# From the second superblock on: token sums of squares as split products with a block of ones and a diagonal, and z gates of two attentions placed elsewhere

## The chip, the cores and the metric

The kernel runs on one core of a Trainium2 chip. The core has a matrix engine (TensorE, PE in the profile, with its weight loads listed apart as PEld), a vector engine (VectorE, DVE), an activation engine (ScalarE, ACT), a general engine (GpSimd, POOL) and a queue processor that here only issues transfers (SyncE, SP). Matrix results land in PSUM, everything else lives in SBUF, inputs and outputs in HBM. The metric is the device time of one execution in microseconds: 2292.9 us, the median of three runs before the change (2291.53 to 2294.29).

## What is computed

The reference is one layer of a hybrid decoder on 2048 tokens of width 1024, all in float32. Cut to the parts that bear on the change:

```python
h = rms_norm(x, norm_g)
p = h @ w_in                       # split into r,k,v,w,a,z_a | q,sk,sv,z_b | xq,z_c | gates
y_a = rwkv7_mix(...)   * silu(z_a) # 8 heads x 64
y_b = sliding_window_sink_attn(...) * silu(z_b)   # 8 q heads x 64, window 128
y_c = memory_cross_attn(...)        * silu(z_c)   # 4 heads x 128, 256 memory tokens
merged = sum(sigmoid(gate_i) * (y_i @ w_proj_i))
x = x + merged @ w_out
# inside rwkv7_mix, per head of 64 channels:
kk = k * k_k;  kk = kk / max(norm(kk), 1e-12)
# inside both attentions, per head (64 or 128 channels):
q = q * rsqrt(mean(q*q) + eps) * g
```

So three places need, per token and head, a sum of squares over the head's channels: the RWKV keys, the queries of the windowed attention, and the queries of the cross attention. (The windowed keys and the memory keys need one too; the change leaves those alone.)

## The kernel before

Tokens go in four superblocks of 512 (`sb` 0 to 3). Activations are kept transposed, channels on the 128 partitions and the 512 tokens along the row. Each projection of `h` to 128 channels (`proj`, L462) is a sum of 24 matmuls of 128 by 128 by 512: float32 operands are split into a high part in the type float32r and a remainder in the same type, and three products high-high, high-low and low-high are added (`gemm3`, L425). The split weights (tiles `whl`) come from HBM: in superblock 0 the raw weights are loaded, split by ACT (L411) and DVE (L412) and written back to a kept copy; in later superblocks the kept copy is loaded (L407).

In each superblock two streams of work are woven. `stream_r` is the RWKV branch: two groups of two head pairs, each group `rwkv_prep` twice, then `rwkv_inverse` (a serial loop on DVE, L754 to L756), then `rwkv_chain` (eight dependent steps). `stream_f` is all the rest: four `cross_head`, `swa_kv`, four `swa_pair` woven with the first output projections (`merge(2)`), `merge(1)`, and eight gates. After both come the split of the RWKV outputs, `merge(0)` and `output`.

The order in which the program writes these steps isn't the order in which an engine runs them. `order` (L276) takes all instructions, estimates each one's time by a table of its own (`cost_PE`, `cost_DVE` and so on), and lays them out by list scheduling: an engine takes, of the instructions that are ready at that time, the one that was written first (its rank, with corrections). That order is then fixed for each engine. Buffers are taken in the order written: each pool of tiles with one name has a fixed number of places, and a tile can be opened only when it is first in its pool's queue (`room`, L197). The pools that matter here are `g2` (11 places of 128 by 512, used by both attentions, by the z gates and by the output), `gt` (2 places, used by the gates of the merges), `rt` (6 places, the scratch of the RWKV stream), and in PSUM `mm` (2 places, all projections), `as_` (2 places, sums and scores of the attentions) and `rw` (2 places, the RWKV stream).

A token's sum of squares is made like this: ACT squares the 128 by 512 tile, and `tok_stat` (L468) takes each of four 128-token slices of the squares as the stationary operand in plain float32 and multiplies it by a narrow constant, `bones` (128 by 2, one column for each half of the partitions) or `ones1` (128 by 1). The results have tokens on the partitions. In `rwkv_prep` (L666 to L674) four small DVE instructions place them by head into `dk` and clamp them. In `cross_head` (L898 to L902) and `swa_pair` (L995 to L999) one DVE copy brings them to `rs`, and POOL makes the inverse root (`rpow`, L391).

The z gate of a head is `silu2` (L869): a projection, a tanh on ACT and one DVE instruction, into a `g2` tile. In `cross_head` it stands after the product with the values (L938), in `swa_pair` after the products with the values (L1056).

Of the kernel before, what the change touches and what calls it, by code (L numbers as in the profile page):

```python
# [9 lines left out]
F32 = mybir.dt.float32  # L10
F32R = mybir.dt.float32r
BF16 = mybir.dt.bfloat16
I32 = mybir.dt.int32
AF = mybir.ActivationFunctionType
ALU = mybir.AluOpType
AX = mybir.AxisListType
# [3 lines left out]
TB = 512  # L20
NG = 11
NRT = 6
SCRATCH = 1024
RAW = 3
C = 64
NC_ = TB // C
# [7 lines left out]
B_R, B_K, B_V, B_WA, B_ZA, B_Q, B_SK, B_SV, B_ZB, B_XQ, B_ZC, B_G = 0, 4, 8, 12, 13, 17, 21, 22, 23, 27, 31, 35  # L34
# [250 lines left out]
def build(tc, A, nsb=4):  # L285
    nc = tc.nc
    es = ExitStack()
    V, S, G, PE = nc.vector, nc.scalar, nc.gpsimd, nc.tensor

    def pool(name, bufs, **kw):  # L290
        return es.enter_context(tc.tile_pool(name=name, bufs=bufs, **kw))
# [5 lines left out]
    rp = pool("rp", 1)  # L297
    yp = pool("yp", 4)
    mp = pool("mp", 9)
    gp_ = pool("gp", NG)  # L300
    bp = pool("bp", 1)
    cp = pool("cp", 1)
    xp = pool("xp", 1)

    def g2(dt=F32, shape=(128, TB)):
        return gp_.tile(list(shape), dt, name="g2")
# [6 lines left out]
    def rw_ps():  # L313
        return ps.tile([128, 512], F32, name="rw", bufs=2)

    def s_ps():
        return ps.tile([128, 512], F32, name="as_", bufs=2)

    def o_ps():
        return ps.tile([128, 512], F32, name="oo", bufs=1)  # L320
# [10 lines left out]
    def const(name, shape, src=None):  # L331
        t = (bp if name == "ident" else fp if name == "eye32" else cp).tile(shape, F32, name="c_" + name)
        nc.sync.dma_start(t, A[name] if src is None else src)
        return t
# [6 lines left out]
    ident = const("ident", [128, 128])  # L341
# [17 lines left out]
    def pcol(name, i=0):  # L359
        o, w = PV[name]  # L360
        return pv[:, o + i:o + i + 1]
# [13 lines left out]
    def dcol(name, i=0):  # L375
        return dv[:, DV[name][0] + i:DV[name][0] + i + 1]
# [27 lines left out]
    def wblock(src, key=None):  # L404
        w = wp.tile([128, 2, 512], F32R, name="whl")
        if key in kept:
            nc.sync.dma_start(w.bitcast(F32), kept[key])  # L407
            return w[:, 0], w[:, 1]
        raw = wp.tile([128, 512], F32, name="raw", bufs=RAW)
        nc.sync.dma_start(raw, src)  # L410
# [51 lines left out]
    def proj(blk, hT, n=TB):  # L462
        o = mm_ps()
        gemm3(o[:, :n], [(w, (hT[0][:, k, :n], hT[1][:, k, :n])) for k, w in enumerate(wtiles(A["w_in"][blk], 8, ("in", blk)))])
        return o


    def tok_stat(sq, nh, ntile, out):  # L468
        rhs = bones if nh == 2 else ones1
        for i in range(ntile):  # L470
            PE.matmul(out[:, i * nh:(i + 1) * nh], sq[:, i * 128:(i + 1) * 128], rhs, start=True, stop=True)

    ones2 = bp.tile([128, 128], F32R, name="ones2")
    S.activation(ones2.rearrange("p (a b) -> p a b", a=2), bones.unsqueeze(2).to_broadcast([128, 2, 64]), AF.Copy)
    ones1 = cp.tile([128, 1], F32, name="ones1")
    V.memset(ones1, 1.0)

    def bcast_T(out, st, nh, ntile):

        w = 128 // nh  # L480
        rep = tmp()[:, :ntile * 128]
        V.tensor_copy(rep.rearrange("p (a b) -> p a b", b=w), st[:, :ntile * nh].unsqueeze(2).to_broadcast([128, ntile * nh, w]))
        for i in range(ntile):
            PE.transpose(out[:, i * 128:(i + 1) * 128], rep[:, i * 128:(i + 1) * 128], ident)
# [127 lines left out]
    def chunks(t):  # L612
        return t.rearrange("p (c t) -> p c t", t=C)

    def shift(o, blk, mu, omu, sb, tag, bufs=1):
        t = rp.tile([128, TB], F32, name=tag, bufs=bufs)
        S.activation(t, o, AF.Copy, scale=omu)
        V.scalar_tensor_tensor(t[:, 1:], o[:, :TB - 1], mu, t[:, 1:], op0=ALU.mult, op1=ALU.add)
        V.scalar_tensor_tensor(t[:, 0:1], carry[sb % 2][:, blk:blk + 1], mu, t[:, 0:1], op0=ALU.mult, op1=ALU.add)
        V.tensor_copy(carry[1 - sb % 2][:, blk:blk + 1], o[:, TB - 1:TB])  # L620
        return t

    def tmp(tag="rt", bufs=NRT):
        return rp.tile([128, TB], F32, name=tag, bufs=bufs)

    EV, OD = slice(0, 64), slice(64, 128)
# [3 lines left out]
    def rwkv_prep(p, i, Z, dk, Nc, sb, hT, lwla, group):  # L630
# [11 lines left out]
        k = shift(kp, B_K + p, pcol("mu_k", p), dcol("omu_k", p), sb, "rk_")  # L642
# [20 lines left out]
            pend.pop(0)()  # L663

        yield 10.317
        sq = tmp()  # L666
        S.activation(sq, k, AF.Square, scale=pcol("k_k", p))
        st = rw_ps()
        tok_stat(sq, 2, 4, st)
        sums, own = st[:, :8].rearrange("p (a e) -> p a e", e=2), dk[:, i].rearrange("p (a o) -> p a o", o=2)  # L670
        for e, h in ((0, EV), (1, OD)):
            for o, at in ((0, EV), (1, OD)):
                V.tensor_scalar(own[h, :, o], sums[at, :, e], 1e-24, None, op0=ALU.max)
        V.reciprocal(dk[:, i], dk[:, i])  # L674
        G.tensor_copy(AB[:, :, C:], gmask[:, C:].unsqueeze(1).to_broadcast([128, NC_, C]))
        G.tensor_tensor(AB[:, :, :C], gmask[:, :C].unsqueeze(1).to_broadcast([128, NC_, C]), dk[:, i].unsqueeze(2).to_broadcast([128, NC_, C]), op=ALU.mult)
# [189 lines left out]
            pend.append(rest)  # L866
        yield 10.587

    def silu2(blk, hT):  # L869

        o = proj(blk, hT)
        t = g2()
        S.activation(t, o, AF.Tanh, scale=0.5)
        V.scalar_tensor_tensor(t, t, 1.0, o, op0=ALU.add, op1=ALU.mult)
        return t
# [10 lines left out]
    def cross_head(h, sb, hT, yh, yl):  # L886
        km = rp.tile([128, 2, M], F32R, name="km", bufs=2)
        nc.sync.dma_start(km.bitcast(F32), Kd[h])
        vm = rp.tile([128, 2, 128], F32, name="vm", bufs=2)
        nc.sync.dma_start(vm, Vd[:, :, h * 128:(h + 1) * 128])  # L890
        o = proj(B_XQ + h, hT)
        qh, ql = g2(F32R), g2(F32R)
        S.activation(qh, o, AF.Copy)
        V.tensor_tensor(ql, o, qh.bitcast(F32), op=ALU.subtract)
        sq = g2()
        S.activation(sq, o, AF.Square)
        yield 1.717
        st = s_ps()  # L898
        tok_stat(sq, 1, 4, st)
        rs = xp.tile([128, 8], F32, name="st8", bufs=2)  # L900
        V.tensor_copy(rs[:, :4], st[:, :4])
        rpow(rs[:, :4], rs[:, :4], 128 * EPS)  # L902
        mx = xp.tile([128, 8], F32, name="mx", bufs=2)
        sps = []
        for t2 in range(2):
            sp = s_ps().rearrange("p (a m) -> p a m", a=2)
            for i in range(2):
                tk = slice((2 * t2 + i) * 128, (2 * t2 + i + 1) * 128)
                gemm3(sp[:, i], [((qh[:, tk], ql[:, tk]), (km[:, 0], km[:, 1]))])
            V.tensor_reduce(mx[:, 2 * t2:2 * t2 + 2], sp, axis=AX.X, op=ALU.max)  # L910
            sps.append(sp)
        V.scalar_tensor_tensor(mx[:, :4], mx[:, :4], -1.0, rs[:, :4], op0=ALU.mult, op1=ALU.mult)
        prs = []
        for t2 in range(2):
            pr = g2(shape=(128, 2, M))
            for i in range(2):
                q = 2 * t2 + i
                S.activation(pr[:, i], sps[t2][:, i], AF.Exp, scale=rs[:, q:q + 1], bias=mx[:, q:q + 1],
                             accum_out=mx[:, 4 + q:5 + q])
            prs.append(pr)  # L920
        dn = xp.tile([128, 8], F32, name="dn", bufs=2)
        V.tensor_scalar(dn[:, :4], mx[:, 4:], 2.0, None, op0=ALU.mult)
        V.reciprocal(dn[:, :4], dn[:, :4])
        yield 5.667
        oo = o_ps()
        for t2 in range(2):
            pt = s_ps().rearrange("p (k i t) -> p k i t", k=2, i=2)
            for i in range(2):
                q = 2 * t2 + i
                V.tensor_scalar(prs[t2][:, i], prs[t2][:, i], dn[:, q:q + 1], None, op0=ALU.mult)  # L930
                for kt in range(2):
                    PE.transpose(pt[:, kt, i], prs[t2][:, i, kt * 128:(kt + 1) * 128], ident)
            pts = g2(shape=(128, 2, 256))
            S.activation(pts.rearrange("p k t -> p (k t)"), pt.rearrange("p k i t -> p (k i t)"), AF.Copy)
            for kt in range(2):
                PE.matmul(oo[:, t2 * 256:(t2 + 1) * 256], vm[:, kt], pts[:, kt], start=kt == 0, stop=kt == 1)  # L936
        yield 3
        z = silu2(B_ZC + h, hT)  # L938
        V.tensor_tensor(z, oo, z, op=ALU.mult)
        split_y(z, yh, yl, "c", h, sb)  # L940
        yield 6.427
# [40 lines left out]
    def swa_pair(j, sb, hT, yh, yl):  # L982
        o = slice(sb * TB, (sb + 1) * TB)
        qp = proj(B_Q + j, hT)
        sq = g2()
# [7 lines left out]
            V.tensor_tensor(q[l], qg[h], q[h].bitcast(F32), op=ALU.subtract)  # L993
        yield 5.067
        st = s_ps()  # L995
        tok_stat(sq, 2, 4, st)
        rs = xp.tile([128, 8], F32, name="st8", bufs=2)
        V.tensor_copy(rs, st[:, :8])
        rpow(rs, rs, 64 * EPS)  # L999
        g = j // 2  # L1000
        mx = xp.tile([128, 4, 4], F32, name="mxs", bufs=2)
# [28 lines left out]
        V.tensor_scalar(dn, dn, 2.0, None, op0=ALU.mult)  # L1030
        V.reciprocal(dn, dn)
        yield 4
        Ps = []
        for b in range(4):
            m0 = m0s[b]
# [17 lines left out]
                    behind(m, prev or last, not prev)  # L1053
                    prev = m
        yield 4
        z = silu2(B_ZB + j, hT)  # L1056
        V.tensor_tensor(z, ops_, z, op=ALU.mult)
        split_y(z, yh, yl, "b", j, sb)
        yield 6
# [54 lines left out]
    def x_norm(sb):  # L1114
        t = hT_tiles()
        norm_T(4, pcols("norm_g"), *t, x0)
        return t
# [32 lines left out]
    hT = x_norm(0)  # L1150
# [3 lines left out]
    for sb in range(nsb):  # L1154
# [51 lines left out]
        if rb is not None:  # L1206
            hT = x_cols(sb + 1, rb)
# [94 lines left out]
```

## Time and profile before

| | |
|---|---|
| median of three runs | 2292.9 us |
| profiled execution, its own time | 2291.46 us |
| its span, first to last instruction | 2289.7 us |
| PE busy | 2251.8 us, 98% |
| PEld busy | 1832.9 us, 80% |
| DVE busy | 1481.7 us, 65% |
| ACT busy | 901.1 us, 39% |
| POOL busy | 149.5 us, 7% |
| mean granted TensorE clock | 0.995 |

The busy time of an engine is the union of its instructions' times. A matmul's end is modelled, and neighbours overlap: a dense matmul's record lasts some 0.39 us, but the next one starts 0.23 us after it. So what a matmul costs the engine is read from start to start in the timeline, and its record's length is not its cost. A float32 matmul leaves two records, so that four instructions of `tok_stat` show as eight. In a timeline row the first number is the start and the second the length, in us, of all the instructions merged into the row. In a row of a group of instructions the last two numbers are busy time in us and mean ns of one.

### The profile page before, as it was taken

Reading aid. Unit: us, or ns where it says so; the run is one execution under the profiler, and the core shown is the slowest. Engines: PE = TensorE matmul, PEld = TensorE weight load, DVE = VectorE, ACT = ScalarE, POOL = GpSimd, SP = SyncE. Lnnn points to the kernel's source line nnn. Section 1 sums busy time; section 2 is a strip of 40 time slices with the busy share of each in tenths; the row PEclk is TensorE's granted clock in tenths of the full one; section 3 lists DMA queues with packets and bytes.
Section 4 is the critical chain, followed back from the end, with each engine's and each line's share of the span. In section 5 each row is a group of like instructions: output and inputs, shape, how many; then the busy total and the mean of one; then the engine's idle time right before and its main releaser. Section 6 shows DMA issues by size and latency. Waiting matters only on the chain.

```text
span 2289.7 us, 37168 instructions
## 1 busy us (share of the span) xinstructions
PE 2251.8 (98%) x13900; PEld 1832.9 (80%) x13900; DVE 1481.7 (65%) x3798; ACT 901.1 (39%) x1971; POOL 149.5 (7%) x209
## 2 busy tenths in 40 slices
PE   8999999999999999999999999999999999999999
PEld 6878778778788788878888878887887887887887
DVE  7799789774458766953435966784244696686312
ACT  6654564545243443433214344332222434434210
POOL 1000110000000010000000001000000001000000
PEclk9999999999999999999999999999999999999999
DMA  7766556589834344446773433445675434343555
GB/s 241 265 210 230 174 178 222 208 288 335 312 135 159 128 140 152 152 155 232 236 254 125 152 122 135 149 148 186 230 251 184 152 131 165 120 153 117 210 193 192
DMA packets 146227, 430.56 MB, mean 188 GB/s; under 512 B 16641, under 2 KB 21121, under 8 KB 146049
## 3 DMA queue, kind: packets, MB, share of 16 engines
q1 hardware_dynamic: 129920, 398.83, 50.4%
q10 hardware_dynamic: 16128, 29.37, 3.8%
q8 instruction: 110, 1.80, 0.3%
q14 instruction: 69, 0.56, 0.1%
HBM read 333.24 MB, written 94.90 MB: 187 GB/s over the span
## 4 chain that ended last, share of the span: by engine, by line
PE 82%; DVE 10%; DMA 3%; ACT 2%; issue 2%; POOL 2%; SPq 0%; ACTq 0%; DVEq 0%; POOLq 0%
PE mm L429 20%; PE mm L431 20%; PE mm L430 19%; PE rw L706 2%; PE rw L827 1%; DVE whl L412 1%; PE oo L1052 1%; PE rw L820 1%; PE mm L1100 1%; PE oo L936 1%; PE mm L1098 1%; PE mm L1099 1%; PE rw L812 1%; POOL var L398 1%; DMA g<-in_x 1%
## 5 line engine op out<-in xcount | busy, mean ns | idle before, releaser
L429 PE MATMUL mm<-hH,whl 128*128 128x512 f32 x1888 | 753.3, 399 | 0.6 <-ACT gt L1065 0.6
L431 PE MATMUL mm<-hH,whl 128*128 128x512 f32 x1888 | 750.9, 398 | 0.0
L430 PE MATMUL mm<-hL,whl 128*128 128x512 f32 x1888 | 749.1, 397 | 0.0
L431 PEld LDWEIGHTS mm<-hH,whl 128*128 128x128 f32 x1888 | 355.6, 188 | 71.7 <-issue 0.7
L429 PEld LDWEIGHTS mm<-hH,whl 128*128 128x128 f32 x1888 | 355.9, 189 | 70.7 <-ACT gt L1065 1.2
L430 PEld LDWEIGHTS mm<-hL,whl 128*128 128x128 f32 x1888 | 355.7, 188 | 69.1 <-issue 0.5
L411 ACT ACTIVATE whl<-raw 128x512 fp32r<-128x512 f32 x178 | 112.3, 632 | 173.6 <-PE mm L431 98.2
L412 DVE TENSOR_TENSOR whl<-raw,whl 128x512 fp32r<-128x512 f32 x178 | 124.5, 701 | 62.3 <-ACT whl L411 61.2
L429 PE MATMUL mm<-yh,whl 128*128 128x512 f32 x384 | 152.0, 396 | 0.8 <-DVE g L1080 0.7
L430 PE MATMUL mm<-yl,whl 128*128 128x512 f32 x384 | 152.0, 396 | 0.0
L431 PE MATMUL mm<-yh,whl 128*128 128x512 f32 x384 | 150.8, 393 | 0.0
L818 ACT ACTIVATE SP<-Z,Pl 64x64 f32<-64x64 f32 x256 | 89.0, 348 | 117.2 <-DVE Z L828 113.6
L754 DVE STREAM_SHUFFLE ibc<-Nc 128x496 f32<-128x496 f32 (+30 forms) x248 | 113.7, 474 | 0.0
L755 DVE TENSOR_TENSOR ibc<-ibc,Yi 128x496 f32<-128x496 f32 (+30 forms) x248 | 104.9, 423 | 4.2
L1027 ACT ACTIVATE g<-g,mxs,st 128x256 f32<-128x256 f32 (+1 forms) x128 | 74.9, 588 | 79.2 <-DVE mxs L1020 78.9
L1080 DVE SCALAR_TENSOR_TENSOR g<-g,mm 128x512 f32<-128x512 f32 x32 | 21.9, 686 | 128.3 <-PE mm L431 128.3
L756 DVE TENSOR_TENSOR Yi<-Yi,ibc 128x496 f32<-128x496 f32 (+30 forms) x248 | 104.0, 419 | 1.4
L828 DVE SCALAR_TENSOR_TENSOR Z<-rw,Pl,SP 64x64 f32<-64x64 f32 x224 | 63.4, 283 | 44.3 <-PE rw L827 40.7
L429 PEld LDWEIGHTS mm<-yh,whl 128*128 128x128 f32 x384 | 72.1, 188 | 16.9 <-DVE g L1080 1.3
L430 PEld LDWEIGHTS mm<-yl,whl 128*128 128x128 f32 x384 | 72.2, 188 | 14.6
L431 PEld LDWEIGHTS mm<-yh,whl 128*128 128x128 f32 x384 | 72.1, 188 | 14.3
L824 DVE TENSOR_TENSOR Z<-rw,dk 64x128 f32<-64x128 f32 x128 | 36.8, 288 | 64.6 <-PE rw L820 54.5
(1815 smaller groups left out, 3718.3 us busy)
## 6 DMA issues: line engine op xcount, KB each, us to landing
whl<-k SPq DMA_DIRECT2D x486, 512.0 KB, 3.3
k<-whl SPq DMA_DIRECT2D x162, 512.0 KB, 3.2
raw<-in_w_in SPq DMA_DIRECT2D x118, 256.0 KB, 3.7
g<-in_x ACTq DMA_DIRECT2D x32, 256.0 KB, 4.3
out<-g ACTq DMA_DIRECT2D x32, 256.0 KB, 4.0
raw<-in_w_proj SPq DMA_DIRECT2D x24, 256.0 KB, 3.7
rt<-in_x ACTq DMA_DIRECT2D x24, 256.0 KB, 4.9
rt<-in_xt ACTq DMA_DIRECT2D x24, 256.0 KB, 5.7
```

The source lines that it names most:

```text
L411: S.activation(w[:, 0], raw, AF.Copy)
L412: V.tensor_tensor(w[:, 1], raw, w[:, 0].bitcast(F32), op=ALU.subtract)
L429: PE.matmul(out, lh, rh, start=i == 0, stop=False)
L430: PE.matmul(out, lh, rl, start=False, stop=False)
L431: PE.matmul(out, ll, rh, start=False, stop=i == n - 1)
L706: m = PE.matmul(g[:, c], BK[h, c0 + c], Q[h, c0 + c], start=True, stop=True)
L754: V.stream_shuffle(bc[:, :, :w], N_[:, :, s + 1:], [s] * 32)
L755: V.tensor_tensor(bc[:, :, :w], bc[:, :, :w], Y[:, :, s:s + 1].to_broadcast([128, n, w]), op=ALU.mult)
L756: V.tensor_tensor(Y[:, :, s + 1:], Y[:, :, s + 1:], bc[:, :, :w], op=ALU.add)
L818: S.activation(SP[h, i], Z[h, i, e, c], AF.Copy, scale=g[4][h, c:c + 1])
L828: upds = [V.scalar_tensor_tensor(Sst[h, g[0]] if c == NC_ - 1 else Z[h, i, e, c + 1], pS[h, i, e], g[4][h, c:c + 1], SP[h, i], op0=ALU.mul ...
L1027: S.activation(prs[b][:, i, m0:], prs[b][:, i, m0:], AF.Exp, scale=r2[:, b, i:i + 1], bias=mx[:, b, i:i + 1], accum_out=mx[:, b, 2 + i:3 + i])
```

## The change

A new constant `FIRST = 1` selects superblocks 1 to 3; superblock 0 keeps the old sums. In the selected ones each of the three places makes its sums with two new helpers. `spread_sums` splits the squares into a high and a low float32r tile (one ACT copy, one DVE subtraction) and multiplies a constant block of ones (`ones2`, block diagonal by halves, or the new `onesw`, all ones) as the stationary operand by both, 512 tokens wide, so that each partition of the result row holds the sum over its head for every token. To have tokens on partitions again, `half_sums` multiplies the result by a repeated 64-wide identity (`eye64`) and sums over each 64 tokens; in `cross_head` four instructions do the same with the 128-wide identity in one go each, a multiplication with an accumulated sum. `swa_pair` then needs four small copies to place the halves.

In all four superblocks, the z gate of `swa_pair` is written before the probabilities are transposed, and the z gate of `cross_head` takes its tile from `gt` instead of `g2`.

```diff
+FIRST = 1
...
+    onesw = bp.tile([128, 128], F32R, name="onesw")
+    S.activation(onesw, ones1.to_broadcast([128, 128]), AF.Copy)
+    eye64 = cp.tile([128, 64], F32, name="eye64")
+    V.tensor_tensor(eye64, ident[:, :64], ident[:, 64:], op=ALU.add)
+
+    def spread_sums(out, w, sq, hi, lo):
+
+        S.activation(hi, sq, AF.Copy)
+        V.tensor_tensor(lo, sq, hi.bitcast(F32), op=ALU.subtract)
+        PE.matmul(out, w, hi, start=True, stop=False)
+        PE.matmul(out, w, lo, start=False, stop=True)
+
+    def half_sums(d, out, junk):
+
+        j = chunks(junk)
+        V.tensor_tensor(j, chunks(out), eye64.unsqueeze(1).to_broadcast([128, NC_, 64]), op=ALU.mult)
+        V.tensor_reduce(d, j, axis=AX.X, op=ALU.add)
...
@@ rwkv_prep
+        if sb >= FIRST:
+            sq = tmp()
+            S.activation(sq, k, AF.Square, scale=pcol("k_k", p))
+            spread_sums(st, ones2, sq, *(rp.tile([128, TB], F32R, name="rt", bufs=NRT) for _ in range(2)))
+            half_sums(dk[:, i], st, sq)
+            V.tensor_scalar(dk[:, i], dk[:, i], 1e-24, None, op0=ALU.max)
+        else:
...
@@ silu2
-    def silu2(blk, hT):
+    def silu2(blk, hT, t=None):
...
-        t = g2()
+        t = g2() if t is None else t
...
@@ cross_head
+        if sb >= FIRST:
+            spread_sums(st, onesw, sq, *(g2(F32R), g2(F32R)))
+            for i in range(4):
+                tk = slice(i * 128, (i + 1) * 128)
+                V.tensor_tensor_reduce(sq[:, tk], st[:, tk], ident, 1.0, 0.0, ALU.mult, ALU.add, rs[:, i:i + 1])
+        else:
+            tok_stat(sq, 1, 4, st)
+            V.tensor_copy(rs[:, :4], st[:, :4])
...
-        z = silu2(B_ZC + h, hT)
+        z = silu2(B_ZC + h, hT, gp_.tile([128, TB], F32, name="gt", bufs=2))
...
@@ swa_pair
+        if sb >= FIRST:
+            spread_sums(st, ones2, sq, *(g2(F32R), g2(F32R)))
+            d = xp.tile([128, 8], F32, name="dh", bufs=2)
+            half_sums(d, st, sq)
+            for i, h in enumerate((EV, OD)):
+                for o, at in enumerate((EV, OD)):
+                    V.tensor_copy(rs.rearrange("p (b i) -> p b i", i=2)[at, :, i], d.rearrange("p (b o) -> p b o", o=2)[h, :, o])
+        else:
+            tok_stat(sq, 2, 4, st)
+            V.tensor_copy(rs, st[:, :8])
...
         V.reciprocal(dn, dn)
         yield 4
+        z = silu2(B_ZB + j, hT)
         Ps = []
...
         yield 4
-        z = silu2(B_ZB + j, hT)
         V.tensor_tensor(z, ops_, z, op=ALU.mult)
```

More of the change, by code (lines that the diff above doesn't have):

```diff
@@ L665, in rwkv_prep @@
         yield 10.317
-        sq = tmp()
-        S.activation(sq, k, AF.Square, scale=pcol("k_k", p))
         st = rw_ps()
[L669 to L673, printed above, removed]
+        if sb >= FIRST:
[5 more added lines that the diff above has]
+        else:
+            sq = tmp()
+            S.activation(sq, k, AF.Square, scale=pcol("k_k", p))
+            tok_stat(sq, 2, 4, st)
+            sums, own = st[:, :8].rearrange("p (a e) -> p a e", e=2), dk[:, i].rearrange("p (a o) -> p a o", o=2)
+            for e, h in ((0, EV), (1, OD)):
+                for o, at in ((0, EV), (1, OD)):
+                    V.tensor_scalar(own[h, :, o], sums[at, :, e], 1e-24, None, op0=ALU.max)
         V.reciprocal(dk[:, i], dk[:, i])
@@ L898, in cross_head @@
         st = s_ps()
-        tok_stat(sq, 1, 4, st)
         rs = xp.tile([128, 8], F32, name="st8", bufs=2)
-        V.tensor_copy(rs[:, :4], st[:, :4])
+        if sb >= FIRST:
[6 more added lines that the diff above has]
+            V.tensor_copy(rs[:, :4], st[:, :4])
         rpow(rs[:, :4], rs[:, :4], 128 * EPS)
@@ L995, in swa_pair @@
         st = s_ps()
-        tok_stat(sq, 2, 4, st)
         rs = xp.tile([128, 8], F32, name="st8", bufs=2)
-        V.tensor_copy(rs, st[:, :8])
+        if sb >= FIRST:
[6 more added lines that the diff above has]
+        else:
+            tok_stat(sq, 2, 4, st)
+            V.tensor_copy(rs, st[:, :8])
         rpow(rs, rs, 64 * EPS)
```

## The prediction

> **What bounds the kernel now.** I read the page's busy times first, then the busy times by stretch, then who waited for whom on PE.
>
> ```profile
> span 2289.7 us, 37168 instructions
> PE 2251.8 (98%) x13900; PEld 1832.9 (80%) x13900; DVE 1481.7 (65%) x3798; ACT 901.1 (39%) x1971; POOL 149.5 (7%) x209
> PE 82%; DVE 10%; DMA 3%; ACT 2%; issue 2%; POOL 2%; SPq 0%; ACTq 0%; DVEq 0%; POOLq 0%
> ```
>
> PE is busy 98% of the span and holds 82% of the chain that ended last. The stretches tell superblock 0 from the others; the columns are the stretch, its length, and busy time with instruction counts of PE, PEld, DVE, ACT and POOL, then the granted clock and the DMA share.
>
> ```profile
> 60.00:570.00 510.00, 494.89 (x3125) 400.77 (x3124) 408.86 (x1006) 271.02 (x572) 38.90 (x47) 0.98 0.67 233
> 630.00:1125.00 495.00, 493.99 (x3174) 401.74 (x3173) 316.70 (x854) 190.02 (x431) 34.09 (x47) 1.00 0.47 162
> 1185.00:1680.00 495.00, 493.55 (x3173) 401.19 (x3172) 318.06 (x856) 190.79 (x432) 34.11 (x47) 1.00 0.47 162
> 1740.00:2240.00 500.00, 499.02 (x3197) 406.36 (x3196) 310.75 (x839) 180.37 (x409) 31.25 (x41) 1.00 0.44 153
> ```
>
> In superblock 0 PE is idle for 510.00 - 494.89 = 15.1 us, with DVE at 80%. In superblock 1 it is idle for 1.0 us, with DVE at 317 of 495, 64%, and ACT at 38%. The waits of PE from 630 to 2240 us are four rows and 3.1 us in all:
>
> ```profile
> PE rw L856 <- DVE rt L853: 1.6, 3, 0.5
> PE as__16692 L1098 <- DVE g L1105: 0.9, 1, 0.9
> PE mm L429 <- DVE g L1080: 0.4, 1, 0.4
> PE as__11578 L1098 <- DVE g L1105: 0.2, 1, 0.2
> ```
>
> So in the three superblocks where the sums change, PE sets the time almost alone. A microsecond less of work in PE's queue is a microsecond less of span there, as long as the other engines go on feeding it.
>
> **What the old sums cost on PE.** A record's length doesn't tell it, so I take starts. First a sum of `rwkv_prep` and then one of `swa_pair`, in PE's timeline:
>
> ```profile
> 885.49 0.39 PE L429 MATMUL mm<-hH,whl 128*128 128x512 f32 x1
> 885.72 0.39 PE L430 MATMUL mm<-hL,whl 128*128 128x512 f32 x1
> 885.95 0.39 PE L431 MATMUL mm<-hH,whl 128*128 128x512 f32 x1
> 886.18 0.95 PE L471 MATMUL rw<-c_bones,rt 128*128 128x2 f32 x8
> 886.98 0.49 PE L429 MATMUL mm<-hH,whl 128*128 128x512 f32 x1
> 887.31 0.40 PE L430 MATMUL mm<-hL,whl 128*128 128x512 f32 x1
> 887.54 0.40 PE L431 MATMUL mm<-hH,whl 128*128 128x512 f32 x1
> ...
> 905.94 0.39 PE L431 MATMUL mm<-yh,whl 128*128 128x512 f32 x1
> 906.17 0.95 PE L471 MATMUL as__9334<-c_bones,g 128*128 128x2 f32 x8
> 906.98 0.37 PE L1011 MATMUL as__9346<-KsH,g 128*128 128x256 f32 x1
> 907.18 0.28 PE L1011 MATMUL as__9346<-KsL,g 128*128 128x256 f32 x1
> 907.30 0.28 PE L1011 MATMUL as__9346<-KsH,g 128*128 128x256 f32 x1
> ```
>
> Dense matmuls start (886.18 - 885.49)/3 = 0.23 us apart. The eight records of a sum take 886.98 - 886.18 = 0.80 us. The first dense matmul behind them costs more than its neighbours: 887.31 - 886.98 = 0.33 where the next takes 0.23, so 0.10 us is added. In the second place it is 0.81, and 0.20 against 0.12, 0.08 added. A sum thus takes 0.90 us of PE in `rwkv_prep` and 0.89 in the attentions.
>
> **What the new sums cost on PE.** Two dense matmuls of 512 columns from a constant block, and no change between plain float32 and float32r on either side. The same form, already in the kernel with `ones2`, is
>
> ```profile
> L731 PE MATMUL rw<-rt,ones 128*128 128x512 f32 x16 | 6.3, 391 | 0.0
> ```
>
> whose record of 391 ns is that of the dense stream (0.39 above), so I take 0.23 from start to start, 0.46 a sum. Each superblock has 4 + 4 + 4 such sums, three superblocks 12 + 24. Off PE come 12 x (0.90 - 0.46) + 24 x (0.89 - 0.46) = 5.3 + 10.3 = 15.6 us. The count of records falls from 8 to 2 a sum.
>
> The Trainium skill, "TensorE: Matmul & The Clock Gate", section "Back-to-back issue gap", lists about 60 cycles for a matmul of 1 to 64 columns and 518 for one of 512. By that table eight records of two columns would take 8 x 60 = 480 cycles, 0.20 us at its 2.4 GHz, and two wide ones 1036, 0.43 us, so the change would add 36 x 0.23 = 8 us. This trace differs: its eight records take 0.80 us.
>
> **What is added beside PE.** Prices come from rows of the same kind:
>
> ```profile
> L1087 ACT ACTIVATE g<-mB 128x512 fp32r<-128x512 f32 x32 | 20.2, 631 | 45.8 <-DVE mB L1081 42.2 <-DMA rt<-in_xt 3.6
> L1089 DVE TENSOR_TENSOR mB<-mB,g 128x512 fp32r<-128x512 f32 x32 | 22.2, 693 | 6.5 <-ACT g L1087 5.6
> L711 DVE TENSOR_TENSOR AB<-rw,AB 64x512 f32<-64x512 f32 x32 | 22.0, 686 | 7.6 <-PE rw L706 7.1
> L848 DVE TENSOR_REDUCE var<-rt 128x8 f32<-128x512 f32 x16 | 10.6, 682 | 2.1 <-ACT rt L846 2.1
> L673 DVE TENSOR_SCALAR dk<-rw 64x4 f32<-64x4 f32 x64 | 10.2, 159 | 0.9
> L1015 DVE CUSTOM_DVE_ANT_0 g<-as__4381,amask x2: 281/344/406, 393.0 to 393.7; 128x128 f32<-128x128 f32 x1, 128x256 f32<-128x256 f32 x1
> L1015 DVE DVE_READ_ACCUMULATOR2_ANT mxs<- x128: 73/84/103, 206.2 to 2065.2; 128x1 f32 x128
> ```
>
> ACT gets 36 copies of 0.63 = 23 us, 7.6 a superblock. DVE per sum: in `rwkv_prep` 0.69 + 0.69 + 0.68 + 0.16, less the four clamps of 0.16 that go, 1.6 us; in `swa_pair` 0.69 + 0.69 + 0.68 + 4 x 0.16 less a copy, 2.5; in `cross_head` 0.69 + 4 x (0.28 + 0.08) less a copy, 2.0. Four each make 24 us a superblock and 73 in all: DVE goes from 64% to 69% and ACT from 38% to 40% in these stretches. I cost this at nothing in the time, since PE hardly waits for either engine there (3.1 us). If that cover goes, the bound is superblock 0: between 64% and 80% of DVE its idle PE time rises from 1.0 to 15.1 us, 0.9 us a point, so 5 points are 4.4 us a superblock and 13 in all. Superblock 0 also has the weight splits that the others lack, so I take the low end.
>
> The RWKV stream gets longer. A sum of `rwkv_prep` ends some 0.63 + 1.6 - 0.44 = 1.8 us later, 7 us in four of them, and the DVE instructions of the attentions, 18 us, can delay its serial loop. So 7 to 25 us, and how late it may end is seen at the end of superblock 1, where its last product (L863) stands against the first matmul of `merge(0)`:
>
> ```profile
> L863 DVE TENSOR_TENSOR ya<-ya,g x2: 685/686/686, 1048.3 to 1048.9; 128x512 f32<-128x512 f32 x2
> ...
> 1112.75 0.48 PE L429 MATMUL mm<-yh,whl 128*128 128x512 f32 x1
> ```
>
> The slack is 1112.75 - 1049.6 = 63 us, filled on PE by `merge(1)` and the gates. The two to four extra tiles of `rt` and `g2` hold up later ones of their pools; their price is in the same bounds.
>
> **The z gates** move no work onto or off PE: 24 matmuls, a tanh, a DVE product and the two weight loads on SP are issued as before, in all four superblocks. In `swa_pair` the loads and the projection now stand ahead of the probabilities' transposes, and the four `P_` tiles queue behind z in `g2`, so that the copies into them (and the products with the values) can't be made before z's tanh. z's projection runs beside the eight exponentials of the pair: 24 x 0.23 = 5.5 us against 8 x (0.59 + 0.19), 6.3 us, by
>
> ```profile
> L1027 ACT ACTIVATE g<-g,mxs,st 128x256 f32<-128x256 f32 x120 | 71.0, 594 | 77.2 <-DVE mxs L1020 76.9
> L1027 ACT ACTIVATION_READ_ACCUMULATOR g<-g,mxs,st 128x1 f32 x128 | 24.4, 190 | 0.0
> ```
>
> That is a cover, so I take 0. In `cross_head` z leaves `g2`, and `gt` is free then, as its gates come later. The bound on both sides is the largest wait that PE has in superblock 0, for the scaled probabilities of a cross head, which may go or come again:
>
> ```profile
> PE as__1903 L932 <- DVE g L930: 3.5, 1, 3.5
> ```
>
> The three instructions for `onesw` and `eye64` run once, while PE waits for the first inputs; 0, at most 1 us.
>
> **Sum.** 2291.5 (profiled execution) - 15.6 = 2275.9. That execution lies 1.4 us under the median of the runs, so for the median 2292.9 - 15.6 = 2277.3, and I say 2277. Bounds of the unknown terms: + 13 for DVE and the pools, + 1 for the constants, 3.5 either way for the z gates.
>
> **Rivals.**
>
> *DVE eats most of it.* The denser DVE delays the evacuation of the two `mm` places and PE stalls as in superblock 0. For it: DVE peaks, 53 of 60 us in the stretch from 690 to 750. Against it: PE is busy 60.00 of 60 us in that very stretch.
>
> ```profile
> 690.00:750.00 60.00, 60.00 (x326) 50.24 (x326) 53.08 (x137) 23.06 (x53) 4.65 (x7) 1.00 0.46 156
> ```
>
> With half to all of the 13 us, 2284 to 2290.
>
> *The sums hold `as_` too long (slower).* The sum's place is one of two in `as_`, and the scores that follow need both. It is now given back after the split and the DVE products: in `swa_pair` 0.63 + 0.69 + 0.69 where a copy of 0.16 stood, in `cross_head` 0.63 + 0.69 + 1.4; 1.9 and 2.6 us later, 12 x 1.9 + 12 x 2.6 = 54 us over 24 heads. If PE has nothing else in its queue at those places, from 15.6 / 54 = 29% exposed the kernel gets slower, and at half exposed it stands at 2277 + 27 = 2304. For it: at the start of a superblock the weights of a cross head's sum already wait for the square,
>
> ```profile
> 1199.29 0.97 PEld L471 LDWEIGHTS as__11848<-ones,g 128*128 128x128 f32 x8 [0.52 <-ACT g L896]
> ```
>
> and the planned order is fixed, so a late sum holds all behind it. Against it: PE shows no other wait for the attentions in superblocks 1 to 3, and projections stand ready to fill.
>
> *PE pays by columns.* If the old sums cost only their few columns, the change adds two dense matmuls, 36 x 0.46 = 16.6 us, 2309. This is the mechanism behind the skill's table above. The starts of the rows speak against it at every place looked at; 1 in 100.
>
> *More gain.* The z gates and the replanned order take away waits of superblock 0 too, 3.5 to 8 of its 15 us: 2269 to 2273.
>
> **Chances.** The forecast itself, 2274 to 2282: 0.60. DVE eats most: 0.16, of which 0.04 ends within 0.2%. More gain: 0.11. Slower by the `as_` places or another stall of the fixed order: 0.09. Between them, no change: 0.03. By columns: 0.01. A change of 0.2% is 4.6 us, about what a measurement of this kernel can tell from no change: under 2288.3 is faster, over 2297.5 slower. Faster is 0.60 + 0.12 + 0.11 = 0.83, same 0.07, slower 0.10. The range leaves out the slower cases and the ends of the others: 2269 to 2290.
>
> **What would show it.** Right: 72 new matmul records of 128 by 512 with the ones blocks in superblocks 1 to 3, 0.46 us a pair from start to start; PE's busy time down by some 16 us, DVE's up by some 73 to 1555, ACT's by 23 to 924; PE's waits from 630 us on still under 6 us; each later superblock some 5 us shorter. Wrong: PE waits at L1011, at the new sums or at the cross scores adding up to over 10 us; a `merge(0)` that waits for the RWKV stream; or dense pairs that cost more than 0.46 us.

## The result, and the profile after

The changed kernel takes 2283.32 us, median of 6 runs (2281.28 to 2284.49), against 2292.22 for the kernel before in the same comparison: a ratio of 0.9961, 95% interval 0.9948 to 0.9974, 8.9 us less. The forecast was 2277 and 15.6 us less. So the direction held, the time lies in the range of 2269 to 2290, just outside the narrower 2274 to 2282 that had most of the chance, and some 7 us of the expected gain are missing.

The page of the changed kernel, in the lines that answer to those shown of before (a line of `after` lies up to 39 further down: `gemm3` is L430 to L432 now, the new sums' matmuls L487 and L488, the cross heads' transposes L963, silu2's tanh L898 and product L899):

```profile
span 2282.2 us, 36933 instructions
PE 2241.2 (98%) x13684; PEld 1814.2 (79%) x13684; DVE 1541.3 (68%) x3967; ACT 916.9 (40%) x2006; POOL 148.6 (7%) x209
PE 70%; DVE 12%; ACT 3%; DMA 2%; issue 1%; POOL 0%; SPq 0%; ACTq 0%; DVEq 0%; POOLq 0%
```

PE's busy time is down by 10.6 us, where the prediction had some 16, and its records by 216 = 36 x 6, eight records of each old sum for two of each new one. Busy time by stretch, columns as in the prediction:

```profile
60.00:570.00 510.00, 496.94 (x3133) 400.61 (x3133) 410.89 (x1012) 271.49 (x575) 37.48 (x47) 0.99 0.68 236
630.00:1125.00 495.00, 493.16 (x3118) 398.22 (x3117) 337.40 (x911) 196.98 (x444) 34.09 (x47) 1.00 0.50 164
1185.00:1680.00 495.00, 493.17 (x3119) 398.35 (x3118) 342.55 (x919) 199.49 (x448) 34.08 (x47) 1.00 0.50 164
```

DVE is at 337 of 495, 68% in superblock 1, and PE still busy 99.6% of it. PE's waits in superblocks 1 to 3, 630 to 2235 us:

```profile
PE rw L837 <- DVE Z L853: 1.1, 3, 0.4
PE as__8859 L487 <- ACT g L485: 0.8, 1, 0.8
PE as__19199 L487 <- ACT g L485: 0.8, 1, 0.8
PE as__14029 L487 <- ACT g L485: 0.8, 1, 0.8
...
PE rw L761 <- DVE carry L638: 0.7, 3, 0.2
```

All of these waits come to 6.0 us, against 3.1 before. Once a superblock a new sum waits 0.8 us for the copy of its high part. Nothing else of size shows, and yet the gain is short. Where it is missing is seen when the span is cut at the last matmul of each `output`. For superblocks 0 and 1 the rows of that line tell it, since the last matmul there is that of the last `as_` tile; first the kernel before, then the changed one:

```profile
L1100 PE MATMUL as__6424<-whl,mB x8: 389/389/389, 613.0 to 625.4; 128*128 128x512 f32 x8
...
L1100 PE MATMUL as__11578<-whl,mB x8: 389/389/389, 1165.0 to 1178.8; 128*128 128x512 f32 x8
```

```profile
L1139 PE MATMUL as__6428<-whl,mB x8: 389/389/390, 616.3 to 628.3; 128*128 128x512 f32 x8
...
L1139 PE MATMUL as__11638<-whl,mB x8: 389/389/395, 1165.0 to 1178.8; 128*128 128x512 f32 x8
```

Superblock 0 ends 2.9 us later than before, and superblock 1 is 2.9 us shorter, so that both kernels stand at 1178.8. All the gain of the span comes behind that point. Cut so, the profiles of all kernels of this study are (us; each from the timeline's last matmul of `output`, with its record of 0.39 us; one execution each; differences in the text can be off by 0.1 from rounding):

| kernel | sums | cross z in | pair z | sb 0 | sb 1 | sb 2 | sb 3 |
|---|---|---|---|---|---|---|---|
| before | old | g2 | late | 625.8 | 553.4 | 554.5 | 552.4 |
| after | new | gt | early | 628.7 | 550.5 | 550.1 | 549.3 |
| e1_sums_only | new | g2 | late | 626.1 | 553.7 | 554.4 | 552.3 |
| e2_z_only | old | gt | early | 628.7 | 554.6 | 555.9 | 553.5 |
| e3_pair_z_only | old | g2 | early | 619.0 | 555.0 | 555.2 | 553.9 |
| e4_cross_z_only | old | gt | late | 631.1 | 552.2 | 553.4 | 551.6 |
| x1_sums_cross_z | new | gt | late | 633.3 | 547.6 | 549.1 | 547.4 |
| x2_sums_pair_z | new | g2 | early | 621.6 | 554.4 | 554.7 | 553.2 |
| x3_split_by_block | new | gt in 1 to 3 | early in 0 | 621.7 | 547.8 | 548.9 | 547.2 |
| x4_sums_12_places | new | g2 of 12 | late | 656.1 | 554.0 | 553.9 | 552.4 |
| y1_probs_out_of_queue | new | g2, pts in gt | late | 631.8 | 550.9 | 551.2 | 549.7 |
| y2_no_cross_sums | new but in cross | g2 | late | 624.7 | 551.4 | 551.9 | 550.9 |
| y4_diag_twice | new, diagonal twice | gt | late | 632.3 | 552.4 | 550.9 | 549.5 |
| y3_split_all_sums | new in 0 too | gt in 1 to 3 | early in 0 | 640.7 | 548.3 | 549.1 | 547.2 |

Two things tell how far such lengths can be trusted. In superblocks 1 to 3 the granted clock is 1.00 in all of these profiles, and kernels with the same order there agree within 0.7 us (x1, x3 and y3). In superblock 0 executions of one order differ by up to 2.7 us (e3, x2 and x3), so the 2.9 us of the changed kernel are little more than that scatter, though e2, with the same order there, repeats them.

### The profile page after: what moved, and what is told of

It reads as the page before. It is cut to its first block, busy times and chain, and to the rows that moved or that the text cites. A ratio compares the mean times of both kernels' runs of the same rounds, so it can differ in the third digit from the quotient of the medians.

```text
span 2282.2 us, 36933 instructions
## 1 busy us (share of the span) xinstructions
PE 2241.2 (98%) x13684; PEld 1814.2 (79%) x13684; DVE 1541.3 (68%) x3967; ACT 916.9 (40%) x2006; POOL 148.6 (7%) x209
## 4 chain that ended last, share of the span: by engine, by line
PE 70%; DVE 12%; ACT 3%; DMA 2%; issue 1%; POOL 0%; SPq 0%; ACTq 0%; DVEq 0%; POOLq 0%
PE mm L431 17%; PE mm L430 17%; PE mm L432 16%; PE rw L731 1%; DVE ibc L779 1%; PE mm L1139 1%; PE mm L1137 1%; PE mm L1138 1%; PE rw L852 1%; PE oo L1092 1%; DVE ibc L780 1%; PE oo L967 1%; PE rw L845 1%; DVE Yi L781 1%; PE rw L837 1%
## 5 line engine op out<-in xcount | busy, mean ns | idle before, releaser
L430 PE MATMUL mm<-hH,whl 128*128 128x512 f32 x1888 | 751.1, 398 | 4.6 <-DVE g L899 3.8
L432 PE MATMUL mm<-hH,whl 128*128 128x512 f32 x1888 | 747.4, 396 | 0.0
L430 PEld LDWEIGHTS mm<-hH,whl 128*128 128x128 f32 x1888 | 355.7, 188 | 76.7 <-DVE g L899 4.3
L432 PEld LDWEIGHTS mm<-hH,whl 128*128 128x128 f32 x1888 | 355.8, 188 | 68.6
L430 PE MATMUL mm<-yh,whl 128*128 128x512 f32 x384 | 152.8, 398 | 1.4 <-DVE g L1119 1.4
L432 PE MATMUL mm<-yh,whl 128*128 128x512 f32 x384 | 151.3, 394 | 0.0
L1104 ACT ACTIVATE gt<-mm 128x512 f32<-128x512 f32 x64 | 37.8, 591 | 129.3 <-PE mm L432 129.2
L430 PEld LDWEIGHTS mm<-yh,whl 128*128 128x128 f32 x384 | 72.1, 188 | 16.6 <-DVE g L1119 2.5
L432 PEld LDWEIGHTS mm<-yh,whl 128*128 128x128 f32 x384 | 72.1, 188 | 14.8
```

Of the source, the lines that this page charges most:

```text
L430: PE.matmul(out, lh, rh, start=i == 0, stop=False)
L432: PE.matmul(out, ll, rh, start=False, stop=i == n - 1)
L1104: S.activation(t, gp, AF.Tanh, scale=0.5)
```

## The experiments

Each ratio below is to the kernel before as it was measured in the same comparison: 2289.86 us for the kernels e1 to e4, 2291.14 for x1 to x4, and 2290.28 for y1 to y4.

**The parts apart.** The first four kernels do the sums alone, the z gates alone, and each z gate alone. With `FIRST = 4` all superblocks keep the old sums.

```diff
# e1_sums_only: the changed kernel with
-        z = silu2(B_ZC + h, hT, gp_.tile([128, TB], F32, name="gt", bufs=2))
+        z = silu2(B_ZC + h, hT)
# and silu2(B_ZB + j, hT) back behind the products with the values
```

> The sums of the changed kernel, with both z gates as in the kernel before. Superblock 0 then has the instructions of the kernel before, but for two constants. Theory A (the sums bring the whole gain in superblocks 1 to 3, some 10 us, and the z gates lose about 3 us in superblock 0): superblock 0 ends near 626 us as before, and the time is 10 to 13 us under the kernel before. Theory B (the z gates carry part of the gain in the later superblocks): 5 to 8 us under it. Theory C (the z gates do nothing and the 3 us of superblock 0 are the scatter of executions): 9 us under it, as the changed kernel.

Measured: 2293.94 us, ratio 1.0019 (1.0010 to 1.0028). No faster than before, by a kernel with the same 216 fewer matmul records: the runs are 0.2% slower, and the span of the profiled execution is 2290.0 us against 2289.7. None of the three theories had that. Superblock 0 is as before (626.1), and each later one takes the old time to 0.3 us: the sums alone gain nothing.

```diff
# e2_z_only: the changed kernel with
-FIRST = 1
+FIRST = 4
```

> Both z gates as in the changed kernel, all sums as in the kernel before (the two new constants are made and unused). Theory A: 2 to 4 us over the kernel before, all of it in superblock 0. Theory B: 1 to 4 us under it, gained in superblocks 1 to 3. Theory C: within 1 us of it.

Measured: 2295.91 us, ratio 1.0025 (1.0017 to 1.0034). Superblock 0 loses the 2.9 us of the changed kernel, and the later ones lose 1.1 to 1.4 each, which no theory had. Neither part gains, and both together do. Theory B is right in that the z gates carry a part, but not as an addition: they let the sums gain. On top of them the sums bring 4.0, 5.8 and 4.2 us a superblock, 14.0 in all, near the forecast of 15.6.

```diff
# e3_pair_z_only: e2_z_only with the cross gate's tile from g2 again
# e4_cross_z_only: e2_z_only with the pair's z gate late again
```

> Only the z gate of the windowed attention is written ahead of the transposes; the cross gate's tile and all sums as before. If the loss of superblock 0 comes from this gate (PE waits 3.8 us at 304 us of the changed kernel for a z gate's DVE product), Theory A gives 2 to 4 us over the kernel before here and a wait of the same kind; otherwise within 1 us.

> Only the cross gate's tile is taken from the two places of the merge gates; the pair's z gate and all sums as before. If this part frees the scratch pool, superblock 0 gets shorter by up to 3.5 us (the wait at the last cross head's transposes goes); if it is neutral, within 1 us of the kernel before; if it causes the loss of superblock 0, 2 to 4 us over it.

Measured: e3 2288.54 us, ratio 0.9996 (0.9987 to 1.0004); e4 2296.0, ratio 1.0028 (1.0019 to 1.0038). The early gate of the pair shortens superblock 0 by 6.8 us and lengthens each later one by 0.7 to 1.6. The cross gate's tile does the reverse, 5.3 us more in superblock 0 and 0.8 to 1.2 less in each later one. For superblock 0 the expectation for e3 looked for a loss and there is a gain; that for e4 named a loss as its third case, of 2 to 4 us, and it is larger. The two don't add in superblock 0 (-6.8 and +5.3 against +2.9 together): each edit lets `order` lay out all of it anew.

**Which gate lets the sums gain.** In the kernel with the sums alone, PE's waits in superblocks 1 to 3 are 14.2 us in all, 11.1 more than in the kernel before, most of the 15.6 that should have been gained. They begin like this:

```profile
PE as__12880 L963 <- DVE g L961: 1.6, 1, 1.6
PE as__18050 L963 <- DVE g L961: 1.5, 1, 1.5
PE as__7710 L963 <- DVE g L961: 1.5, 1, 1.5
```

Each is the last cross head of a superblock, PE idle until its probabilities are scaled. Around that wait, the rows of PE and then those of ACT:

```profile
742.31 0.39 PE L432 MATMUL mm<-hH,whl 128*128 128x512 f32 x1
744.25 0.63 PE L963 MATMUL as__7710<-c_ident,g 128*128 128x128 f32 x4 [1.54 <-DVE g L961]
```

```profile
744.91 0.60 ACT L965 ACTIVATE g<-as__7710 128x512 f32<-128x512 f32 x1 [2.05 <-PE as__7710 L963]
745.43 0.60 ACT L965 ACTIVATE g<-as__7721 128x512 f32<-128x512 f32 x1
745.93 0.59 ACT L898 ACTIVATE g<-mm 128x512 f32<-128x512 f32 x1
746.41 0.60 ACT L987 ACTIVATE g<-mm 128x512 f32<-128x512 f32 x1
```

The dense stream stops at 742.3. ACT is free, and two finished projections wait: z's, done at 736.5 and read by the tanh at 745.93, and the windowed keys', done at 742.7 and read by the square (L987) at 746.41 (the last 24 dense matmuls into `mm` are the keys', the 24 before them z's). They hold both `mm` places, so PE has no place for another projection. z's tanh goes straight behind the two copies into `pts` (L965), which stand ahead of it in `g2`. The next kernels test that.

```diff
# x1_sums_cross_z: the changed kernel, pair's z gate late again
# x2_sums_pair_z: the changed kernel, cross gate's tile from g2 again
```

> The new sums with the cross gate's tile in the merge gates' two places; the pair's z gate as in the kernel before. Theory D (with z in g2 the two extra tiles of a cross head's sum make the g2 queue too short, so cross heads come late and PE waits at their transposes; taking z out of it is what lets the sums gain): superblocks 1 to 3 take 549 to 551 us each, no PE wait at the cross transposes, and superblock 0 some 631 us as with that gate's tile alone; about 2282 in the profile's span. Theory E (the pair's earlier z gate is what lets them gain): superblocks 1 to 3 stay at 553 to 554 us with the waits of the sums alone.

> The new sums with the pair's z gate written early; the cross gate's tile from g2 as before. Theory D: superblocks 1 to 3 stay at 553 to 556 us each with waits at the cross transposes, and superblock 0 is some 619 us. Theory E: 549 to 551 us each.

Measured: x1 2282.42 us, ratio 0.9959 (0.9945 to 0.9973); x2 2288.06, ratio 0.9988 (0.9979 to 0.9996). It is the cross gate's tile: with it the later superblocks take 547.6, 549.1 and 547.4 us in x1 and 549.3 to 550.5 in the changed kernel, without it 552.3 to 554.7 whatever the pair's gate does. Against the same gates with old sums (e4) the sums gain 4.6, 4.3 and 4.2 us, 13.1 in all. The same place in x1, ACT first and then PE:

```profile
742.86 0.60 ACT L898 ACTIVATE gt<-mm 128x512 f32<-128x512 f32 x1 [3.94 <-PE mm L432]
...
752.20 0.60 ACT L965 ACTIVATE g<-as__7710 128x512 f32<-128x512 f32 x1 [3.19 <-PE as__7710 L963]
```

```profile
751.33 0.39 PE L432 MATMUL mm<-hH,whl 128*128 128x512 f32 x1
751.56 0.60 PE L963 MATMUL as__7710<-c_ident,g 128*128 128x128 f32 x4
```

The tanh now runs 9.3 us ahead of the copies, as soon as z's projection is done, and the transposes follow the dense stream with no gap.

**Number of places or order in the queue.**

```diff
# x4_sums_12_places: e1_sums_only with
-NG = 11
+NG = 12
-RAW = 3
+RAW = 2
```

> The new sums with both z gates as before, and g2 with 12 places in place of 11. To make room one of three buffers of raw weights goes, which only superblock 0 uses, so it is read by superblocks 1 to 3. Theory D: they take 549 to 551 us each, and the PE waits at the cross transposes (2.5 us a superblock with the sums alone) go. If the waits come from the denser DVE: they stay, 553 to 554 us each.

Measured: superblocks 1 to 3 take 554.0, 553.9 and 552.4 us, and the waits stay:

```profile
PE as__12880 L963 <- DVE g L961: 1.5, 1, 1.5
PE as__7710 L963 <- DVE g L961: 1.5, 1, 1.5
PE as__18050 L963 <- DVE g L961: 1.5, 1, 1.5
```

A twelfth place doesn't help. It changes nothing in those superblocks: ACT and DVE run the same instructions in the same order as in e1, and PE does up to the matmuls of `output`. So theory D's reason, a queue too short, finds no support, though it had the right gate (the sums open two more tiles, and two more places weren't run). The time of the whole, 2320.0 us, ratio 1.0122 (1.0105 to 1.0140), is superblock 0's, which is 30 us longer with two raw buffers.

```diff
# y1_probs_out_of_queue: e1_sums_only with
-            pts = g2(shape=(128, 2, 256))
+            pts = gp_.tile([128, 2, 256], F32, name="gt", bufs=2)
```

> The new sums with both z gates as in the kernel before; in place of z, the two transposed probability tiles of a cross head (pts) come from the merge gates' places, so z still uses g2 but no longer stands behind them in its queue. Theory F (z's tanh had to come after both copies into pts, and held one of the two mm places meanwhile; 12 places of g2 couldn't help): the waits at the cross transposes go and superblocks 1 to 3 take 547 to 550 us. Theory G (it is z's own tile, or its number of places, that matters): they stay at 552 to 555 us with those waits.

Measured: 2287.4 us, ratio 0.9989 (0.9980 to 0.9998). The waits at the cross transposes are gone from the list, as theory F said:

```profile
PE mm L430 <- DVE g L899: 4.4, 3, 1.5
PE as__14029 L487 <- ACT g L485: 1.3, 1, 1.3
...
PE as__8859 L487 <- ACT g L485: 1.3, 1, 1.3
```

But the superblocks take 550.9, 551.2 and 549.7, two of them between the two theories' ranges: 2.8, 3.2 and 2.6 us under e1, about half of what the gate's own tile gave (6.1, 5.3, 4.9). In place of the waits that went, PE waits 1.5 us a superblock for z's DVE product, which still frees an `mm` place late, and 1.3, up from 0.7, for a sum's high part. The same place as above, ACT first and then PE, shows why z is still late:

```profile
747.21 0.56 ACT L949 ACTIVATE g<-as__7691,mx,st 128x256 f32<-128x256 f32 x1
747.75 0.60 ACT L898 ACTIVATE g<-mm 128x512 f32<-128x512 f32 x1
```

```profile
749.15 0.50 PE L430 MATMUL mm<-hH,whl 128*128 128x512 f32 x1 [1.48 <-DVE g L899]
```

z's projection was done at 741.5, but its tanh runs straight behind the fourth exponential, which writes the second of the probability tiles that stand ahead of z in `g2`. In x1 it ran ahead of all four. So z's place behind `pts` in the queue is a cause, and without it the wait seen is gone (y1 also leaves two tiles' room in `g2`, which x4 makes an unlikely reason). z's place behind the probabilities is the next of the same kind. How much of the other half that is, and how much comes from the new layout of the whole, wasn't tested.

**Whose chain it is.**

```diff
# y2_no_cross_sums: e1_sums_only with, in cross_head,
-        if sb >= FIRST:
+        if False:
```

> Both z gates as in the kernel before; the new sums in the RWKV keys and the windowed queries, the old sums in the cross heads. If the longer chain of the cross heads' sums is what eats the gain, the eight remaining sums gain 8 x 0.43 = 3.5 us a superblock: 549 to 551 us each, without waits at the cross transposes. If the loss is spread over all sums: 552 to 554.

Measured: 2285.36 us, ratio 0.9983 (0.9974 to 0.9993); 551.4, 551.9 and 550.9 us, two between the two ranges and one at the end of the first. At the cross transposes PE waits 0.3 us a superblock, where e1 waits 1.5 and more:

```profile
PE as__8839 L487 <- ACT g L485: 0.9, 1, 0.9
...
PE as__11990 L963 <- DVE g L961: 0.3, 1, 0.3
```

Eight sums gain 2.0, 2.6 and 1.4 us a superblock, of the 3.5 worked out; one wait of 0.9 at a new sum is in that. Adding the four cross sums (e1) loses 2.3, 2.5 and 1.4 where their PE work alone is 1.7 less. So by this difference, which has the new layout in it, the cross heads' longer chain costs some 3 to 4 us a superblock while z waits behind it, and is the larger part of the loss.

**DVE's load.**

```diff
# y4_diag_twice: x1_sums_cross_z with, in half_sums, once more
+        V.tensor_tensor(j, chunks(out), eye64.unsqueeze(1).to_broadcast([128, NC_, 64]), op=ALU.mult)
+        V.tensor_reduce(d, j, axis=AX.X, op=ALU.add)
```

> The new sums with the cross gate's tile in the merge gates' places and the pair's z gate as before, and the diagonal's product and reduction made twice in the RWKV keys and the windowed queries, the second time with the same result: 8 x 1.38 = 11 us more DVE time a superblock, 2.2 points, and 1.4 us more in each of these chains. By the forecast's bound (0.9 us a point) 2.0 us more a superblock, 549.6, 551.1 and 549.4; if DVE's load costs nothing there, within 0.5 us of 547.6, 549.1 and 547.4.

Measured: 2288.44 us, ratio 0.9991 (0.9982 to 1.0000); 552.4, 550.9 and 549.5 us, that is 4.8, 1.8 and 2.1 over x1, 2.9 in the mean for 11 us of DVE work. The prediction's bound of 0.9 us a point gave 2.0. So eleven more microseconds of DVE in these chains aren't covered. Whether it is the load, the 1.4 us in each chain or the new layout, this kernel doesn't tell.

**A version by superblock.** The pair's early gate is good in superblock 0 and bad later, the cross gate's tile the reverse.

```diff
# x3_split_by_block: the changed kernel with
-        z = silu2(B_ZC + h, hT, gp_.tile([128, TB], F32, name="gt", bufs=2))
+        z = silu2(B_ZC + h, hT, gp_.tile([128, TB], F32, name="gt", bufs=2) if sb else None)
...
+        if not sb:
         z = silu2(B_ZB + j, hT)
...
+        if sb:
+            z = silu2(B_ZB + j, hT)
```

> The new sums; the pair's z gate early in superblock 0 alone, the cross gate's tile from the merge gates' places in superblocks 1 to 3 alone. If the parts of each superblock add (619 us for superblock 0 as with the early pair gate alone, 549 to 550 for each later one): a span of 619 + 3 x 549.5 + 3.5, some 2271 us, and 13 to 18 us under the kernel before. If the pair's early gate is needed in the later superblocks too: 2280 to 2284.

Measured: 2268.68 us (2267.84 to 2271.05), ratio 0.9900 (0.9883 to 0.9917): 22 us under the kernel before and some 14 under the changed one. The parts do add by superblock, since each keeps the layout it has in x1 or e3: the order of PE, ACT and DVE is the same in the traces.

```diff
# y3_split_all_sums: x3_split_by_block with
-FIRST = 1
+FIRST = 0
```

> As the kernel with the z gates split by superblock (2268.7 us), with the new sums in superblock 0 too. There DVE is at 80% and PE idle for 15 us. If PE's work sets superblock 0 too: 3 to 5 us less, 617 to 619 us for it and 2264 to 2266 in all. If DVE sets it: 24 us more of DVE work there at up to 0.9 us a point give 3 to 5 us more, 625 to 627 us, and 2272 to 2274.

Measured: 2290.69 us, ratio 1.0004 (0.9996 to 1.0013). Superblock 0 takes 640.7 us, 19 more than in x3 and far outside both expectations. Its stretch from 60 to 570 us, y3 first and x3 second, and then y3's longest PE wait there:

```profile
60.00:570.00 510.00, 484.87 (x3008) 387.33 (x3008) 418.26 (x1051) 272.57 (x577) 37.85 (x47) 0.98 0.65 226
```

```profile
60.00:570.00 510.00, 498.48 (x3139) 402.11 (x3139) 413.91 (x1017) 274.98 (x580) 37.58 (x47) 0.99 0.68 237
```

```profile
PE as__1929 L963 <- DVE g L961: 6.8, 1, 6.8
```

PE is idle 25.1 us in place of 11.5. The longest wait is again at the last cross head's transposes, with z in `g2` in that superblock, where DVE is at 82%. A kernel with z out of `g2` there and all the new sums wasn't run, so whether z's place or DVE makes this loss stays open.

## Why the prediction was right, and where it was off

*PE bounds superblocks 1 to 3.* Right with a condition. With the cross gate's tile out of the way, 15.6 us less PE work gave 13.1 us less time (x1 against e4). With it in `g2` the same work gave nothing (e1 against before, 0.1 us more over three superblocks). That PE waited for almost nothing before told that its queue was well filled, not that it would be after each chain beside it got longer. That the condition was met is luck as far as the prediction goes: it gave the cross gate's tile no part in the sums' gain.

*The old sums' 0.90 and the new ones' 0.46 us.* Right in the rows:

```profile
1244.26 0.39 PE L432 MATMUL mm<-hH,whl 128*128 128x512 f32 x1
1244.48 0.39 PE L487 MATMUL rw<-rt,ones 128*128 128x512 f32 x1
1244.71 0.39 PE L488 MATMUL rw<-rt,ones 128*128 128x512 f32 x1
1244.93 0.39 PE L430 MATMUL mm<-hH,whl 128*128 128x512 f32 x1
```

The pair takes 1244.93 - 1244.48 = 0.45 us with no step at either side. Not every pair is laid out so well. In superblock 2 of the changed kernel 7 of the 24 matmuls of the new sums take some 0.34 us or more from start to start, where they stand behind plain float32 work or have waited for their operand; the pairs' mean there is 0.55, and more than 0.46 was named as a sign of being wrong. In x1 it is 0.51, some 1.8 us over 36 sums.

*The added DVE and ACT work at nothing.* The sizes were right: DVE's new records less the dropped ones sum to 73.6 us against 73 forecast, though its busy time rose by only 59.6, since records overlap. ACT's copies sum to 22.7 us against 23. The price wasn't always nothing: it lies in the chains (y2, y4), and with z in `g2` it is paid in the cross heads above all. With the cross gate's tile away all of it fits into the 2.5 us that x1 lacks of the 15.6.

*The z gates at 0, at most 3.5 us.* This is the step that failed. The prediction took them for a move without a price. It saw for the pair that a tile behind z in `g2` can't be written before z's tanh, and didn't ask the same of the cross gate, where z itself stood behind other tiles. The cross gate's tile decides whether the sums gain: with new sums it is worth 16.2 us over superblocks 1 to 3 (x1 against e1), with old ones 3.1 (e4 against before). The pair's early gate costs 5.8 us there (after against x1), and 3.8 with old sums (e3 against before). Superblock 0 lost 2.9. So the sum, in place of 15.6: 16.1 gained by the new sums with the cross gate's tile (x1 against before, superblocks 1 to 3), 5.8 given back by the pair's gate, 2.9 lost in superblock 0; to rounding that is 7.5, the difference of the two spans, against 8.9 of the medians. That the pair's cover, exponentials beside z's projection, would make its move free was wrong in those superblocks. Part of it may be more steps between float32r and plain float32: with old sums, superblock 1 has 131 of them into plain float32 with the early gate and 122 without, counted in PE's timeline, which at the prediction's 0.10 us a step would be 0.9 us, an estimate. With new sums it has 109 in both, PE's waits differ by only 1.3 us over three superblocks (6.0 against 4.7), and the loss stays, so the cause is open.

*The slower rival, long chains.* Its mechanism was there and its place wasn't. The sums' longer chain does stall PE, but by the two `mm` places that z's tanh and the next projection hold, not by `as_`. It decides in e1, and the change carries its own remedy.

*DVE eats most* gave 2284 to 2290 and comes nearest in time, but its means, a dense DVE that frees the `mm` places late, isn't what cost the missing 7 us: x1, with the same added work, takes 16.1 us less than before in superblocks 1 to 3.

## What to carry to other kernels

When an edit shortens the work of the bounding engine and lengthens the chain beside it, look for the place that the chain holds: here a tanh stood behind a softmax's tiles in a buffer queue and held a projection's PSUM place all that while, and the sums gained nothing until it got a buffer elsewhere. Parts that look like housekeeping must be run alone and together, since neither of the two parts alone made the kernel faster and both together did. Where a planner lays out each stage anew, choose by stage, and judge by the length of the stage.

## What the runs showed of the hardware that was not expected

One and the same order of instructions gave superblock 0 lengths of 619.0, 621.6 and 621.7 us (e3, x2, x3) and 631.1, 633.3 and 632.3 (e4, x1, y4), while the later superblocks of one order agreed within 0.2 us in x1 and x3 and within 0.7 with y3. And one raw weight buffer less, with one scratch place more, made superblock 0 longer by 30 us (x4 against e1).
